# A two-layer encoder on one core: its scan in chunks of 64, with one matrix per unit made beforehand

## The chip, the cores and the metric

The kernel runs on one core of one Trainium2 chip. The metric is the device time of one execution in microseconds, median of the runs; beside it stands one profiled execution, whose trace is quoted here. The engines are PE (TensorE: matrix products into PSUM; PEld is its weight load), DVE (VectorE), ACT (ScalarE), POOL (GpSimd) and SP, which issues the DMAs.

## The reference

Input and output are 512 positions of 1024 features in float32. Layer 0 normalises, projects to seven groups of features, mixes them by a short convolution and by a 128x128 matrix over positions per group, gates, and projects back. Layer 1 normalises, projects, and has two mixers: a recurrence (forward and backward, 16 heads of 64 features) and a Fourier transform with a linear map; both are gated and projected back, and a last normalisation ends it. The change touches the recurrence alone:

```python
def wkv7_step(state, inp):
    r, w, k, v, a, b = inp
    sa = jnp.einsum('...ij,...j->...i', state, a)
    state = (state * w[..., None, :] + sa[..., :, None] * b[..., None, :]
             + v[..., :, None] * k[..., None, :])
    y = jnp.einsum('...ij,...j->...i', state, r)
    return state, y
...
    init = jnp.zeros((2, bsz, C_HEADS, C_HEAD_DIM, C_HEAD_DIM), jnp.float32)
    xs = (to_scan(r), to_scan(decay), to_scan(k), to_scan(v), to_scan(-kk), to_scan(kk * a))
    _, y = lax.scan(wkv7_step, init, xs)
    y = jnp.moveaxis(y, 0, 2)
    y_sum = y[0] + jnp.flip(y[1], axis=1)
    out = layer_norm(y_sum, lnx_g.reshape(C_HEADS, C_HEAD_DIM),
                     lnx_b.reshape(C_HEADS, C_HEAD_DIM), GN_EPS)
```

## The kernel before, in words

**Order.** The code doesn't call the engines. Each part of the work is a generator (a strand) that yields instructions (`Op`) and the names of things that it waits for; `Plan.run` keeps a rough clock of each engine and always issues the instruction that could start first, of equals that of the strand with the lower rank. Each engine then runs its instructions in that order. The scan (`chain`) has rank 0 and is looked ahead into: `held` keeps engines free for it. The blocks of layer 1's input projection (`block`, 24 products of 512 columns for 128 features) are strands of rank 5, gated by the scan's progress so that they lie between its steps. All instructions are recorded at one line, L367 (L378 in the changed program), so the trace is read by tiles. Tiles come from rings (`get`, `free`): a strand waits until a place of its ring is free. The planner's `took` charges extra where float32 products give way to float32r ones.

**Dense products** are float32r, every operand split into a high and a low part, three products each (`mm3`): `pd_*`, `pe`, `po`. The products of the recurrence are float32, and the trace has two records for each.

**The recurrence** goes over head pairs j = 0 to 7: two heads on 64 partitions each. A unit is a head e of the pair and a direction d, so a pair has four units. The sequence is cut into chunks of C = 32 positions, 16 to a pair, 128 in all. What a pair needs is built while the pair before it is scanned:

- `prep`, `half` (L1014): decays E, and the operands `at`, `bk` (b and k beside each other, by chunk) and `ar` (a and r, one tile per unit and half of the sequence), the latter copied into place by ACT or DVE.
- `sc`: scores of b and k with a and r in a chunk (64x64 tiles, two of them in turn); `masked` (L1053) copies the part that is to be inverted into `M` and masks the rest into `ar`.
- `inverse` (L1127): DVE solves blocks of 16, one matrix to a lane, in 30 short multiplications and additions of `iA` and `iT`; PE joins two blocks to 32 (`iH`, `iTT`, 32x32 tiles).
- `turn` (L1193): PE transposes `bk` (`tb`), ACT copies it into `bs`. `fold` (L1219): the inverse times b (`fb`) and times scores (`fr`), copied back into `bs` and `ar`.

**The scan** (`chain`, L1262). X has, for each unit, 64 rows of state, 32 of corrections and 32 of values. One chunk is a round trip of two products and two DVE instructions:

```python
ops = [V.tensor_tensor(X, pa, ph[:, :, n:n + 1].to_broadcast([P, 4, 64]), ALU.mult)]
ops += [T.matmul(pb[self.uq(e, d), n % 2, :], ar[e][d][n // 8][:, n % 8, 0, :], X[:, 2 * e + d, :], start=True, stop=True) for e, d in ((0, 0), (0, 1), (1, 1), (1, 0))]
ops += [V.copy_predicated(X, self.umask, pb[:, n % 2:n % 2 + 1, :].to_broadcast([P, 4, 64]))]
```

after which `bs` times X (128x64 tiles) and the next values (`c_cen`, 64x32 tiles) go into `pab`, and `outs` multiplies X with `ar` into `py` (128x32 tiles). `outputs` (L1317) copies `py` out, transposes it (`pt`) and adds the directions. `post` normalises and gates.

**PSUM**: four buffers `d` for dense blocks, two `s` for the building, one `py`, one `pab`.

Of the kernel before, what the change touches and what calls it, by code (L numbers as in the profile page):

```python
# [24 lines left out]
C = 32  # L25
NCH = S // C

# rows of the parameter matrix: 128 features each
# [15 lines left out]
def lay_out(inputs):  # L44
    """The arrays of one launch: the inputs laid out in the order of their tiles, and constants of shapes."""
# [21 lines left out]
def tables():  # L67
    """Constants: they depend on shapes alone."""
# [5 lines left out]
    t["cen"] = np.tile(np.eye(64) - 1 / 64.0, (2, 1))  # L74
    r, q = p % 64 // C, p % C
    c = np.arange(C)
    lt, le = q[:, None] < c[None, :], q[:, None] <= c[None, :]
    masks = []
    for d in range(2):
        is_k = (r == 1 - d)[:, None]  # L80
        masks.append(np.concatenate([lt & is_k, le], 1))
    t["masks"] = np.concatenate(masks, 1)
    t["eye32"] = q[:, None] == c[None, :]
    t["halves"] = np.stack([p % 2 == 0, p % 2 == 1, q < 16], 1)
# [10 lines left out]
# tiles with parts that depend on nothing in each other: after how many elements the parts repeat, and their size  # L95
PARTS = {"x23": (2 * D, D), "h1_23": (2 * D, D), "bk": (P, 64), "sq": (2 * S, S), "E": (2 * NCH * (C + 1), NCH * (C + 1)), "vq": (2 * S, S),
         "xw": (2 * S, S), "bs": (2048, 512), "ar": (64, 32), "y": (S, 256)}


@functools.lru_cache(None)  # L100
def parts(at, dims, period, size):
    """The parts that an access touches."""
    found = {at}
    for step, n in dims:
        found = {(a + step * i) % period for a in found for i in range(n)}
    return sorted({a // size for a in found})


class Op:
    """An instruction that is not issued yet: its engine, its call, what it writes and reads, and about how long it takes."""  # L110

    def __init__(self, eng, name, call, a, kw):
# [6 lines left out]
        if eng == "PE":  # L119
            m, n = math.prod(aps[1].shape[1:]), math.prod(aps[2].shape[1:])  # L120
            k, self.round = aps[1].shape[0] / P, aps[1].dtype == F32R
            self.cols = n * k * m / P
            if name == "transpose":
                self.cols *= 2
                self.cost = 0.11
            elif self.round:
                self.cost = n / 2400
            else:
                self.cols *= 4
                self.cost = n / 600 if m == P else 2 * max(m, n) / 1200 if aps[0].start_partition() == 0 else m / 1200  # L130
# [5 lines left out]
        # of what touches a bank of PSUM, one engine waits for another  # L136
# [4 lines left out]
    def where(x):  # L141
        """What it depends on: a tile by quarters of the partitions; of some tiles, their two parts."""
# [3 lines left out]
        if name.startswith("pab"):  # L146
            name = "pa" if x.offset % 384 < 256 else "pb"
# [4 lines left out]
        kind = PARTS.get(re.match("h1_23|x23|[a-z]*", name, re.I)[0])  # L152
# [6 lines left out]
class Plan:  # L159
    """The order of the instructions of many strands, each in its own order: always the instruction that could  # L160
    start first by a rough clock of the engines, of equals the one whose strand matters most. Every engine
    then runs its instructions in this order."""

    TICK, WINDOW, BUSY, SOFT = 3.413, 3.2, 3050.0, 2600.0
    SAFE, URGE = {}, 0.3
# [4 lines left out]
    def __init__(self, tc, nc):  # L170
        self.tc = tc
        self.clock = dict.fromkeys(("PE", "ACT", "DVE", "Pool", "SP"), 0.0)
        self.clock.update(round=False, table=None)
        self.wrote, self.read, self.cols = {}, {}, {}
        self.strands, self.done, self.rings, self.recent = [], set(), {}, deque()
# [10 lines left out]
    def unit(*ops):  # L186
        """Instructions that stay together if they can."""
# [5 lines left out]
    def either(op, other, gain):  # L193
        """An instruction that another engine could do; it does if that ends sooner by more than gain."""
# [6 lines left out]
    def get(self, pool, shape, dt, tag, name, bufs):  # L201
# [196 lines left out]
class K:  # L398
# [665 lines left out]
    def sums(self, j):  # L1064
# [18 lines left out]
        if j > 2:  # L1083
            yield f"X{j - 3}_15"
# [565 lines left out]
```

## Time and profile before

| | |
|---|---|
| Runs, us | 1132.07 median of 3 (1130.79 to 1137.01) |
| Profiled execution, span, us | 1137.8 |
| PE / DVE / ACT / POOL busy | 97% / 62% / 49% / 19% |
| Layer 0 | 0 to 440 us |
| Ramp: layer 1 begins, the first pair is built | 440 to 537 us |
| Scan: 128 chunk steps | 537 to 1072 us |
| Tail: output projection | 1072 to 1138 us |

The span runs from the first to the last instruction of the profiled execution; it lies at the upper end of the runs, 0.5% over their median. Busy PE time includes the draining of products and whatever lies between one product's start and its own end, so PE can be busy and still not issue.

### The profile page before, as it was taken

The numbers are of one execution on the slowest core, as the hardware profiler recorded it, in microseconds if no ns is written. First come the engines' busy times: TensorE is split into PE (matmuls) and PEld (weight loads), VectorE is DVE, ScalarE is ACT, GpSimd is POOL, SyncE is SP. The second block draws the span as 40 slices with busy tenths as digits, with TensorE's granted clock in tenths as the row PEclk, the third lists the DMA queues.
The fourth block names the chain that finished last, engine by engine and source line by source line (L and its number), as shares of the span: only waits on it lengthen the run. The fifth ranks groups of instructions, "written<-read, shape, count | busy, mean of one in ns | idle before, by whom it ended". The sixth has DMA issues, their size and how long they took to land.

```text
span 1137.8 us, 29635 instructions
## 1 busy us (share of the span) xinstructions
PE 1100.6 (97%) x12984; PEld 831.9 (73%) x12984; DVE 707.8 (62%) x1325; ACT 558.7 (49%) x976; POOL 211.9 (19%) x225
## 2 busy tenths in 40 slices
PE   7999999999999999989999999999999999999997
PEld 6988888888888888666666666666656666676786
DVE  6374444434432358897678678788777787856543
ACT  6232222222221156977386485773935847445333
POOL 3021111011010014342113112223222231122100
PEclk9999999999999999999899999999989999999999
DMA  8222222222232332222001101101111111242142
GB/s 288 76 93 93 74 93 94 103 100 93 93 130 93 130 130 84 85 70 72 21 31 48 49 31 48 46 33 39 31 55 41 39 39 41 94 146 85 57 139 111
DMA packets 32610, 91.57 MB, mean 80 GB/s; under 512 B 4960, under 2 KB 7648, under 8 KB 32480
## 3 DMA queue, kind: packets, MB, share of 16 engines
q1 hardware_dynamic: 32480, 89.67, 22.7%
q8 instruction: 102, 1.67, 0.6%
q14 instruction: 28, 0.23, 0.1%
HBM read 81.73 MB, written 7.86 MB: 79 GB/s over the span
## 4 chain that ended last, share of the span: by engine, by line
PE 81%; DVE 8%; ACT 8%; issue 2%; POOL 1%; DMA 0%; SPq 0%; POOLq 0%; DVEq 0%
PE pab L367 9%; PE pe L367 7%; PE po L367 6%; PE pv L367 4%; PE pd_ub L367 4%; PE pd_zb L367 4%; PE pd_xa L367 4%; PE pd_ba L367 4%; PE pd_za L367 4%; PE pd_ca L367 4%; PE pd_k L367 3%; PE pd_zc L367 3%; PE py L367 3%; PE pd_r L367 3%; PE pd_v L367 3%; PE sc L367 2%
## 5 line engine op out<-in xcount | busy, mean ns | idle before, releaser
L367 DVE COPY_PREDICATED X<-umask,pab 128x256 f32<-128x256 uint8 x128 | 56.9, 445 | 53.9 <-PE pab L367 53.2
L367 DVE TENSOR_TENSOR X<-pab,ph 128x256 f32<-128x256 f32 x128 | 54.0, 422 | 44.2 <-PE pab L367 42.8
L367 PE MATMUL pe<-w_e,yh 128*128 128x512 f32 x256 | 81.3, 398 | 0.0
L367 PEld LDWEIGHTS pab<-X,bs 128*64 128x64 f32 x960 | 38.4, 139 | 39.2 <-issue 13.6
L367 PE MATMUL pab<-X,bs 128*64 128x64 f32 x960 | 55.2, 237 | 6.6 <-DVE X L367 6.6
L367 PEld LDWEIGHTS pe<-w_e,yh 128*128 128x128 f32 x256 | 48.0, 188 | 11.6
L367 PE MATMUL pd_zc<-hh,w_zc 128*128 128x512 f32 x128 | 54.3, 435 | 0.9 <-POOL w_zc L367 0.9
L367 PE MATMUL pd_k<-hh,w_k 128*128 128x512 f32 (+1 forms) x144 | 54.2, 409 | 0.0
L367 ACT COPY bs<-tb 64x256 f32<-64x256 f32 x122 | 44.8, 367 | 16.1 <-PE tb L367 14.5
L367 PE MATMUL pe<-w_e,yl 128*128 128x512 f32 x128 | 50.4, 393 | 0.0
L367 PE MATMUL py<-X,ar 128*32 128x64 f32 x1024 | 50.3, 227 | 0.0
L367 PE MATMUL pd_v<-hh,w_v 128*128 128x512 f32 x128 | 50.1, 423 | 0.0
L367 PE MATMUL pd_r<-hh,w_r 128*128 128x512 f32 x128 | 50.0, 425 | 0.0
L367 DVE TENSOR_TENSOR w_e<-wf_e,w_e 128x1024 fp32r<-128x1024 f32 (+1 forms) x18 | 19.0, 1076 | 48.1 <-ACT w_e L367 47.9
L367 DVE TENSOR_TENSOR ar<-sc,c_masks 64x512 f32<-64x512 f32 x64 | 43.9, 686 | 7.6 <-ACT M L367 6.3
L367 PE MATMUL pv<-w_pv,hh 128*128 128x256 f32 x256 | 47.6, 289 | 0.0
L367 PEld LDWEIGHTS pab<-X,ar 128*32 128x32 f32 x1024 | 20.4, 109 | 37.2 <-issue 12.8
L367 ACT CAST w_e<-wf_e 128x1024 fp32r<-128x1024 f32 (+1 forms) x19 | 16.9, 912 | 62.3 <-PE pe L367 54.4
L367 ACT COPY M<-sc 32x256 f32<-32x256 f32 x62 | 37.6, 607 | 16.9 <-PE sc L367 16.1
L367 PE MATMUL pab<-X,ar 128*32 128x64 f32 x1024 | 41.4, 234 | 4.4 <-DVE X L367 4.3
L367 PE MATMUL sc<-ar,bk 64*64 64x64 f32 x1024 | 44.6, 224 | 0.9 <-ACT bs L367 0.9
L367 PEld LDWEIGHTS sc<-ar,bk 64*64 64x64 f32 x1024 | 35.7, 134 | 10.1 <-issue 3.6
(337 smaller groups left out, 2963.3 us busy)
## 6 DMA issues: line engine op xcount, KB each, us to landing
wf_e<-in_w_eo SPq DMA_DIRECT2D x16, 512.0 KB, 3.2
wf_o<-in_w_oo SPq DMA_DIRECT2D x12, 512.0 KB, 4.2
wf_pv<-in_w_ev SPq DMA_DIRECT2D x8, 512.0 KB, 5.6
wf_ub<-in_w_e SPq DMA_DIRECT2D x8, 512.0 KB
wf_zb<-in_w_e SPq DMA_DIRECT2D x8, 512.0 KB, 3.3
wf_xa<-in_w_e SPq DMA_DIRECT2D x8, 512.0 KB
wf_ca<-in_w_e SPq DMA_DIRECT2D x8, 512.0 KB, 3.2
wf_za<-in_w_e SPq DMA_DIRECT2D x8, 512.0 KB
```

What stands on the lines that cost most here:

```text
L367: i = op.call(*op.a, **op.kw)
```

## The change

A chunk has C = 64 positions: eight to a pair, 64 in all. For each unit and chunk one 128x128 matrix is made beforehand (`gq`): its right half takes X to the next state, its left half takes X to the outputs. A step of the scan is one DVE multiplication, `G` times X and the next values into `pa`, and X times `G` into `py`, all on 128x64 tiles (`c_cen` is padded with zeros to 128 rows). The outputs come feature-major and summed over the directions in PSUM, so the transposition after the scan is gone. The copy of corrections (`COPY_PREDICATED`) is gone too.

The building changes: `scores` makes the matrix to invert (`sm`), then products of a with k and the state (`sa`) and of b with r and the state (`sz`), 128 columns wide; `inverse` goes one step further, joining two inverses of 32 to one of 64 (`iTB`, `iG`, `iTJ`); `fold` multiplies with the inverse (`sp`) and sums four terms into each G (`sg`). b, k and r stay in one tile `ops` with an identity behind them.

The planner now charges for a change of tile shape on PE and prefers to stay with the shape that it has. `SLACK`, in chunks, is 2 for 4. PSUM has three `d` and three `s` buffers; a pass that needs two `s` waits for both.

```diff
-C = 32
+C = 64
...
+            self.mode = tuple(next(x for x in (32, 64, P) if x >= y) for y in (aps[1].shape[0], P if name == "transpose" else m))
...
-            cost += 0.09 * (op.round and not clock["round"])
-            clock["round"] = op.round
-            if self.cols.get(int(t / self.TICK) - 1, 0.0) < 3060:
+            if op.mode != clock["mode"]:
+                cost += self.SWITCH
+            clock["mode"] = op.mode
+            if self.cols.get(int(t / self.TICK) - 1, 0.0) < self.COLD:
...
+        if op.eng == "PE" and op.mode != self.clock["mode"] and not s[3]:
+            at += self.STAY
...
-                lo = yield from self.get("ll", f"ll{j}_{d}")
+                lo = self.ll[d]
...
-                                         T.matmul(ps, lo[r], self.xw[d][r, i, :], start=False, stop=True))
+                                         T.matmul(ps, lo[:, i, :], self.xw[d][:, i, :], start=False, stop=True))
...
+    def scores(self, j):
+        T, V, g = self.T, self.V, self.g[j]
...
+        for m in range(8):
+            for b in range(2):
+                for e, d in self.units:
+                    x = at[d][self.cr(e), C * m:C * m + C].rearrange("p (h c) -> p h c", h=2)
+                    yield T.matmul(ps[e][self.quarter(d, b), m, :], self.chunk(j, d, e, 0, m)[:, 32 * b:32 * b + 32], x[:, ::-1, :] if b else x, start=True, stop=True)
+        for e in range(2):
+            yield self.copy(mt[:, 8 * e:8 * e + 8, :], ps[e])
...
+            for m in range(4):
+                for e, d in self.units:
+                    yield T.matmul(ps[d][self.half_(e), m, :], at[d][self.cr(e), C * (4 * h + m):C * (4 * h + m) + C], self.ahead(j, d, e, 1, 4 * h + m), start=True, stop=True)
+            for e in range(2):
+                yield V.tensor_tensor(am[:, e, :, 0:C], ps[e][:, :, 0:C], self.masks[:, None, 5 * C:6 * C].to_broadcast([P, 4, C]), ALU.mult)
+                yield self.copy(am[:, e, :, C:2 * C], ps[e][:, :, C:2 * C])
...
+                    yield T.matmul(ps[e][self.half_(d), m, :], self.chunk(j, d, e, 0, n), self.ahead(j, d, e, 2, 7 - n if d else n), start=True, stop=True)
...
+        for n in range(16):
+            for r in rows[1::2]:
+                yield T.matmul(pt[r, n, :], H[r, n, :], Dt[r, n, :], start=True, stop=True)
+        for q, r in enumerate(rows):
+            yield self.copy(Ti[r, :, q % 2 * 32:q % 2 * 32 + 32], ps[r])
...
+                yield T.matmul(ps[q, n, :], mt[r, n, 32:64], Ti[r, n, 0:32], start=True, stop=True)
...
+                yield T.matmul(ps[r, n, :], B[r, n, :], H[r, n, :], start=True, stop=True)
...
+                    yield T.matmul(ps[d][self.half_(e), m, :], Ti[self.half_(d), 8 * e + 4 * h + m, :], zz[self.half_(d), e, m, :], start=True, stop=True)
...
+                            same.append((ps[e][self.cr(e), u, :], self.ident[self.cr(e), self.cr(e)], x))
+                            same.append((ps[e][self.cr(e), u, :], am[self.half_(e), d, n % 4, C:C2], y))
+                            other.append((ps[e][self.sr(e), u, :], self.chunk(j, d, e, 1, n), x))
+                            other.append((ps[e][self.sr(e), u, :], am[self.half_(e), d, n % 4, 0:C], y))
+                for k in range(8):
+                    for q in ((0, 0), (1, 1), (0, 1), (1, 0)):
+                        out, l, x = todo[q][k]
+                        yield T.matmul(out, l, x, start=k == 0, stop=k == 7)
...
+                        yield V.tensor_tensor(G[:, e, u, 0:C], ps[e][:, u, 0:C], x, ALU.mult)
+                    yield self.copy(G[:, e, :, C:C2], ps[e][:, :, C:C2])
...
+                ops = [V.tensor_tensor(X, pa, ph[:, :, m:m + 1].to_broadcast([P, 4, 64]), ALU.mult)]
+                if m < NCH - 1:
+                    ops += [T.matmul(pa[self.cr(e), 2 * e + d, :], G[:, e, 2 * (m % 2) + d, C:2 * C], X[:, 2 * e + d, :], start=True, stop=True) for e, d in units]
+                    ops += value(m + 1)
+                for e, d in units:
+                    t = C * (NCH - 1 - m if d else m)
+                    ops.append(T.matmul(py[self.cr(e), t:t + C], X[:, 2 * e + d, :], G[:, e, 2 * (m % 2) + d, 0:C], start=m == 0 and d == 0, stop=m == NCH - 1 and d == 1))
...
-            dp, sp, yp, cp = (self.pool(ctx, name, n, PSUM) for name, n in (("dense", 4), ("short", 2), ("outs", 1), ("chain", 1)))
+            dp, sp, yp, cp = (self.pool(ctx, name, n, PSUM) for name, n in (("dense", 3), ("short", 3), ("outs", 1), ("chain", 1)))
```

The order on PE at a chunk step. In a row, the product's tile is left of the arrow, its inputs right of it, then the output's size (partitions x columns); x4 stands for four alike. Before, chunk 13 of the third pair (the second visit of that step; the first one, four products `pab<-X,ar`, stands six dense products ahead):

```order
L367 MATMUL pd_k_6855<-hh,w_k_6749 128x512
L367 MATMUL pab<-X_13_6886,bs_3280 64x64 x4
L367 MATMUL pab<-c_cen,vq_5412 32x64 x4
L367 MATMUL py_8_6779<-X_13_6886,ar_011_5406 32x64
L367 MATMUL py_8_6779<-X_13_6886,ar_111_5408 32x64
L367 MATMUL py_8_6779<-X_13_6886,ar_001_5405 32x64
L367 MATMUL py_8_6779<-X_13_6886,ar_101_5407 32x64
L367 MATMUL pd_k_6855<-hh,w_k_6748 128x512
```

Now, chunk 2 of the fourth pair, PE again:

```order
L378 MATMUL za_1_6721<-xw_3336,ll_105 128x512
L378 MATMUL pa<-X_2_6727,gq_01_6581 64x64 x4
L378 MATMUL pa<-c_cen,vq_5038 64x64 x4
L378 MATMUL py_6582<-gq_01_6581,X_2_6727 64x64 x4
L378 MATMUL sz_00_6713<-ops_3233 64x128
L378 MATMUL sz_00_6713<-ops_3241 64x128
L378 MATMUL sz_01_6714<-ops_3233 64x128
L378 MATMUL sz_01_6714<-ops_3241 64x128
```

The visit with X and `ar` is gone, the twelve products that are left have one tile shape, and what stands behind them are products of the next pair's building rather than dense ones.

The order on PE in the building of the second pair, before, where the joint `iTT` is made:

```order
L367 MATMUL pab<-X_5_4684,ar_100_3450 32x64
L367 MATMUL iTT_4788<-iHs_4681,iDt_4661 32x32 x26
L367 MATMUL pab<-X_5_4684,bs_3224 64x64 x4
L367 MATMUL pab<-c_cen,vq_3295 32x64 x4
L367 MATMUL iTT_4788<-iHs_4681,iDt_4661 32x32 x19
L367 MATMUL pd_r_4631<-hh,w_r_4369 128x512
L367 MATMUL pd_r_4631<-hl,w_r_4369 128x512
L367 MATMUL pd_r_4631<-hh,w_r_4370 128x512
```

Now, the second pair again (`dz` is the inverse, `iB` and `iG1s` are copies out of PSUM, `ss` the sums of squares of the pair after):

```order
L378 MATMUL iTT_5149<-iHs_4762,iDt_4746 32x32 x64
L378 MATMUL iTB_5150<-iDt_4746,iHs_4762 32x32 x32
L378 MATMUL iG_5260<-dz_3253,mt_4361 32x32 x32
L378 MATMUL iTJ_5301<-iG1s,iB_5257 32x32
L378 MATMUL ss_5306<-sq_5240,ones 32x256 x2
L378 MATMUL iTJ_5301<-iG1s,iB_5257 32x32 x31
L378 MATMUL ss_5306<-sq_5240,ones 32x256 x2
L378 MATMUL sp_00_5351<-zz_0_4672,dz_3253 64x128
```

A pass that was cut into pieces by scan steps and dense products now runs whole, and passes that read each other's results stand behind each other.

## Rows read from the trace of the kernel before

**Rows 1.** The page's engine shares: busy us (share of the span), instructions.

```profile
PE 1100.6 (97%) x12984; PEld 831.9 (73%) x12984; DVE 707.8 (62%) x1325; ACT 558.7 (49%) x976; POOL 211.9 (19%) x225
```

**Rows 2.** Engine time by stretch: us; busy and count per engine; clock, DMA, GB/s.

```profile
0.00:440.00 440.00, 430.84 (x2147) 363.56 (x2148) 199.79 (x265) 137.01 (x191) 56.42 (x61) 1.00 0.32 111
440.00:537.00 97.00, 91.59 (x1016) 66.36 (x1015) 82.91 (x149) 76.31 (x144) 30.22 (x34) 1.00 0.23 80
537.00:1072.00 535.00, 518.91 (x9567) 354.28 (x9567) 397.98 (x872) 318.12 (x600) 123.64 (x129) 0.98 0.15 51
```

**Rows 3.** Waits in 537 to 1072 us: who for whom, us in total, times, longest.

```profile
DVE X L367 <- PE pab L367: 96.0, 152, 2.4
...
PE pab L367 <- DVE X L367: 10.9, 13, 1.8
PE iTT L367 <- DVE iHs L367: 2.2, 2, 1.8
```

**Rows 4.** PE in order of time, 703 to 707 us: start, length, what, count.

```profile
703.01 0.40 PE L367 MATMUL pd_v<-hl,w_v 128*128 128x512 f32 x1
703.24 0.39 PE L367 MATMUL pd_v<-hh,w_v 128*128 128x512 f32 x1
703.57 0.32 PE L367 MATMUL pab<-X,ar 128*32 128x64 f32 x8
703.81 0.50 PE L367 MATMUL pd_k<-hh,w_k 128*128 128x512 f32 x1
704.16 0.39 PE L367 MATMUL pd_k<-hl,w_k 128*128 128x512 f32 x1
...
705.07 0.40 PE L367 MATMUL pd_k<-hh,w_k 128*128 128x512 f32 x1
705.40 0.45 PE L367 MATMUL pab<-X,bs 128*64 128x64 f32 x8
705.78 0.32 PE L367 MATMUL pab<-c_cen,vq 64*32 64x64 f32 x8
706.03 0.42 PE L367 MATMUL py<-X,ar 128*32 128x64 f32 x8
706.38 0.51 PE L367 MATMUL pd_k<-hh,w_k 128*128 128x512 f32 x1
706.73 0.40 PE L367 MATMUL pd_k<-hl,w_k 128*128 128x512 f32 x1
```

**Rows 5.** PE in order of time: unbroken passes, each with the row behind it.

```profile
512.66 2.08 PE L367 MATMUL sc<-ar,bk 64*64 64x64 f32 x64 [0.86 <-ACT bs L367]
514.67 0.49 PE L367 MATMUL zw<-xw,lh 128*128 128x512 f32 x1
...
567.46 0.45 PE L367 MATMUL py<-X,ar 128*32 128x64 f32 x16
567.72 0.31 PE L367 MATMUL pab<-X,ar 128*32 128x64 f32 x8
569.72 0.66 PE L367 MATMUL tb<-c_ident,bk 128*128 128x128 f32 x4
...
723.35 1.10 PE L367 MATMUL fb<-bs,Ti 32*32 32x64 f32 x64 [0.92 <-ACT Ti L367]
724.37 0.50 PE L367 MATMUL pd_r<-hh,w_r 128*128 128x512 f32 x1
728.42 0.75 PE L367 MATMUL fr<-ar,Ti 32*32 32x32 f32 x64 [0.41 <-ACT bs L367]
729.10 0.51 PE L367 MATMUL pd_zc<-hh,w_zc 128*128 128x512 f32 x1
```

**Rows 6.** DVE groups: shapes, count, busy us, mean ns, idle before and releaser.

```profile
L367 DVE COPY_PREDICATED X<-umask,pab 128x256 f32<-128x256 uint8 x128 | 56.9, 445 | 53.9 <-PE pab L367 53.2
L367 DVE TENSOR_TENSOR X<-pab,ph 128x256 f32<-128x256 f32 x128 | 54.0, 422 | 44.2 <-PE pab L367 42.8
L367 DVE TENSOR_TENSOR ar<-sc,c_masks 64x512 f32<-64x512 f32 x64 | 43.9, 686 | 7.6 <-ACT M L367 6.3
```

More of the change, by code (lines that the diff above doesn't have):

```diff
@@ L220, in free, with both @@
         next(s for s in self.rings[tag] if s[0] is not None and s[0].tensor.name == t.tensor.name)[1] = True
+    def both(self, tag):
+        ring = self.rings.get(tag)
+        while ring and sum(s[1] for s in ring) < 2:
+            yield tag, "both", ring, 2
     def credit(self, tag, n):
@@ L298, in settle @@
                             break
-                    elif not (w in self.done if isinstance(w, str) else any(x[1] for x in w[2])):
+                    elif not (w in self.done if isinstance(w, str) else sum(x[1] for x in w[2]) >= w[3]):
                         break
@@ L479, in splits @@
             if key.startswith("pv") and key.endswith("_0"):
[L480 to L481 removed]
+                at = []
+                for tag in ("G", "ops"):
+                    at.append((tag, (yield from self.get(tag, f"w{tag}_{key}", shape, F32R))))
+                tiles = [t for _, t in at]
             elif key in (f"o0_{OUTS[-1]}", f"o1_{OUTS[-2]}"):
@@ L996, in build @@
             yield f"prep{j}_0"
-            g["bk"] = yield from self.get("bk", f"bk{j}")
+            g["ops"], g["at"], g["G"] = [], [None, None], []
+            for d in range(2):
+                g["ops"].append((yield from self.get("ops", f"ops{j}_{d}")))
             g["sq"] = yield from self.get("sq", f"sq{j}", [P, 2, S])
@@ L1182, in inverse @@
-        Ti = g["T"] = yield from self.get("Ti", f"Ti{j}")
-        for n in range(NCH):
-            for q in range(4):
-                r = slice(32 * q, 32 * q + 32)
-                yield T.matmul(ps[r, n, :], Dt[r, n, :], H[r, n, :], start=True, stop=True)
+        yield from self.plan.both("s")
+        ps = yield from self.get("s", f"iTT{j}", [P, 16, 32])
+        pt = yield from self.get("s", f"iTB{j}", [P, 16, 32])
+        for n in range(16):
+            for r in rows:
+                yield T.matmul(ps[r, n, :], Dt[r, n, :], H[r, n, :], start=True, stop=True)
@@ new lines, in inverse @@
+        B = yield from self.get("Dn", f"iB{j}", [P, 16, 32])
+        for r in rows[1::2]:
+            yield self.copy(B[r], pt[r])
+        self.free("s", pt)
+        ps = yield from self.get("s", f"iG{j}", [P, 16, 32])
+        for n in range(16):
+            for d in range(2):
+                r, q = rows[2 * d], rows[2 * d + 1]
+                yield T.matmul(ps[q, n, :], mt[r, n, 32:64], Ti[r, n, 0:32], start=True, stop=True)
+        self.free("q", mt)
+        H = yield from self.get("F", f"iG{j}s", [P, 16, 32])
@@ new lines, in inverse @@
+        for r in rows[1::2]:
+            yield self.copy(H[r], ps[r])
+        self.free("s", ps)
+        ps = yield from self.get("s", f"iTJ{j}", [P, 16, 32])
+        for n in range(16):
+            for r in rows[1::2]:
+                yield T.matmul(ps[r, n, :], B[r, n, :], H[r, n, :], start=True, stop=True)
+        for r in rows[1::2]:
+            yield self.copy(Ti[r, :, 0:32], ps[r])
+        self.free("s", ps)
+        self.free("Dn", B)
+        self.free("F", H)
+        self.plan.done.add(f"tt{j}")
@@ L1259, in unit_states @@
-        self.plan.done.add("bs")
+        for tag, n in (("ops", 4), ("dz", 2)):
+            got = []
+            for i in range(n):
+                t = yield from self.get(tag, f"{tag}{i}")
+                got.append(t)
+                if tag == "dz":
+                    yield self.G.memset(t, 0.0)
+                else:
+                    for e in range(2):
+                        yield self.G.tensor_copy(t[self.cr(e), 3 * S:], self.ident[self.cr(e), self.cr(e)])
+            self.plan.keep.add(tag)
+            self.free(tag, *got)
```

556 lines of the change are left out of this document (255 added, 301 removed).

## The prediction

> **What bounds the kernel now.** I read the page's line of engine shares first: PE (TensorE) is busy 97% of the 1137.8 us span, DVE 62%, ACT 49% [rows 1]. An average hides stages, so next the table of engine time by stretch [rows 2]. Layer 0 (0 to 440 us) is dense 512-column products; the ramp (440 to 537) makes the first head pair ready; the scan (537 to 1072) is 128 chunk steps with layer 1's projections and the building of the next head pair between them; the tail is dense again. PE is busy 518.9 of 535 us in the scan, DVE 398.0. Third, the waits [rows 3]. DVE waits 96.0 us for PE's `pab`, PE only 10.9 us for DVE's X: the recurrence looks serial, but the engine that ends its wait is nearly always PE, and PE is working through its queue. So the scan's time is a sum of PE time, and halving the number of steps by itself buys nothing. What counts is the PE time that is removed and added.
>
> Fourth, how this PE time is spent, in the order of time [rows 4]. Dense products follow each other every 0.23 us (703.01 to 703.24). At 703.57 a visit of four scan products (128x32 tiles) comes between two dense blocks: from the last dense start, 703.24, to the second dense start after it, 704.16, are 0.92 us. Two dense products are 0.46 of it and the four scan products 0.13 (below); 0.33 go to two changes of tile shape. The second visit of that step, at 705.40, has three shapes: from 705.07 to 706.73 are 1.66 us, less 0.46, less 0.55 for its twelve products, which leaves 0.65 for four changes, 0.16 each. The stretch from 705.78 to 706.03, 0.25 us for four products and one change, gives 0.12. I take **0.15 us a change**, with 0.12 and 0.165 as ends. This is what a row doesn't name: the engine counts as busy there.
>
> **What one small product costs.** From unbroken passes, start to next start, less one change of 0.15 where one stands [rows 5] (two records are one float32 product). Scores `sc`, 64 columns on two tiles: (2.01 - 0.15) / 32 = 0.058 us. `fb`, 64 columns on four tiles: (1.02 - 0.15) / 32 = 0.027. `fr`, 32 columns on four tiles: (0.68 - 0.15) / 32 = 0.017. `py` with eight products in a row on four column tiles: 0.26 / 8 = 0.0325. One tile thus takes about 0.117 us for 64 columns and 0.066 for 32, whatever else runs, and the price is that over the number of different tiles in turn. 128 columns don't occur on small tiles; from 32 to 64 columns 0.05 comes on top, so 0.21 at the least by that slope, 0.234 by doubling; I take 0.22, or 0.055 on four tiles and 0.11 on two. A transposition: four in 0.66, the last end trailing by 0.17 as the dense rows' do, so 0.12.
>
> **The change part by part.** Counts are instructions of the two programs.
>
> *Removed products*: `sc` 512 x 0.058 = 29.7; `fb` 512 x 0.027 = 13.8; `fr` 512 x 0.017 = 8.7; 128 `tb` and 64 `pt` transpositions x 0.12 = 23.0; the scan's `pab<-X,ar` 512 x 0.0325 = 16.6, `pab<-c_cen` 512 x 0.03 = 15.4, `pab<-X,bs` 480 x 0.058 = 27.8, `py` 512 x 0.05 = 25.6 (mostly on two tiles). Sum 161 us.
>
> *Added products*: `sg` 1024 on four tiles x 0.055 = 56.3; `sz` and `sp` 512 x 0.055 = 28.2; `sa` 256 on two tiles x 0.11 = 28.2; `sm` 512 x 0.022 = 11.3 (0.017 to 0.029, four tiles or more); the joints `iTB`, `iG`, `iTJ` 768 on two tiles x 0.033 = 25.3 (0.017 to 0.066, four tiles or one); `pa` 480 and `py` 256 x 0.058 = 42.7. Sum 192 us. So the arithmetic costs **+31 us**: folding more beforehand is more work, not less.
>
> *Changes of tile shape*: 979 in the program before, 309 after. A chunk step had up to six of them, at 128 steps; now its twelve products have one shape (128x64), at 64 steps, and the planner keeps equal shapes together; the 64-row LoRA products are padded to 128 and change nothing any more. 670 x 0.15 = **-100 us** (-80 to -111).
>
> *Waits.* Before, all idle PE time of the scan is 535 - 518.9 = 16 us. After, a head pair is built in 15 passes (`sm`, two `sa`, two `sz`, `iH`, `iTT` with `iTB`, `iG`, `iTJ`, two `sp`, four `sg`), and most read what DVE or ACT takes out of PSUM after the pass before. The price of such a hop with nothing under it is that of `iTT` waiting for `iHs`: 2.2 us in two waits, 1.1 each [rows 3]. In the new order dense blocks cover most; bare are some six in the first pair, where the dense blocks have run out, and one or two in each other pair (the `iG`, `iTJ`, `sp` rows of the change's section). 18 x 1.1 = **+20 us**; the ends are 0 (as tight as now) and +70.
>
> *Beside the path.* DVE loses COPY_PREDICATED 56.9, half of the X multiplications 27.0 and the `ar` masks 43.9 [rows 6], and gets 64 masks of 256 columns at the X row's 0.42 = 27 and 128 of 128 columns, which lie under that price, at most 54: it falls, and stays under PE, which covers it at some 74% as now. ACT loses its copies into `bs`, `ar` and `M`. Eight small loads a pair for `nss` instead of two stand in SP's queue ahead of weights; what waits for them is the inverse of a pair, with the dense blocks of the ramp and a whole pair's period over it, and the weights are three slabs ahead: nothing, while those covers last; if the first inverse started 2 or 3 us later, the ramp would pay that once. Three dense PSUM buffers for four: a block lasts 24 x 0.23 = 5.5 us, so each buffer has two blocks' time to be emptied; nothing. The transform's last two groups now wait for the last chunk; the output projection's other blocks lie over that.
>
> **Sum.** 1137.8 + 31 - 100 + 20 = 1089 us for a profiled execution. The median of the runs before is 1132.07, 0.995 of the profiled span, so 1089 x 0.995 = **1083 us**.
>
> **The rivals.**
>
> *Tiles that share rows work one after the other* (slower). `sg`, `sz` and `sp` count on four 64x64 tiles at once, two on the same 64 rows. If those two took turns, 1536 products would cost 0.11 and not 0.055: +84, so 1173 x 0.995 = 1167 us. For it: no 64x64 pass of the trace has more than two tiles, on different rows. Against it: `pab<-c_cen` has two 64x32 tiles on each half of the rows, and its four products take 0.25 with their change [rows 4], a quarter of one tile's time each. It decides from 0.10 us per product on, where it eats the gain. The Trainium skill ("TensorE: Matmul & The Clock Gate", section on packing small matmuls) says that a weight load overlaps running matmuls only where the row group differs. By that rule this rival would be the forecast and `c_cen` could not be at a quarter; the trace disagrees with it there, which is why its chance is small: 0.07.
>
> *The hops come bare* (no change, or slower). PSUM's three small buffers are taken two at a time, and each must be emptied by DVE and ACT before the pass after next. If ten of a pair's 15 hops were bare, 8 x 10 x 1.1 = 88 instead of 20: 1157, or 1151 us. It decides from some eight bare hops a pair (69 us). For it: the passes are longer and the dense blocks between them come in runs of 24 rather than of 3, so that cover lies in fewer places. Against it: the same planner leaves PE 16 idle us in the scan now, with 14 such passes a pair. The skill ("TensorEngine Tiling", PSUM Bottleneck) warns of this: tiling speeds up the products, not the emptying, which may become the bound. Here DVE and ACT get less to empty, so by the rows it is latency alone that could cost. Chance 0.10, of which 0.04 within half a per cent.
>
> *The scan's latency was the bound after all* (much faster). Then 64 steps of one hop in place of 128 of two would give hundreds of us. PE's 10.9 us of waiting for X speak against it; the most that could be had of all PE waits in the scan is 16 us. With no bare hop at all: 1069, or 1064 us. That is inside my range; below it I leave 0.05, for better-packed `sa` and joints.
>
> *The change doesn't do what it says*: if the order had as many shape changes as before. The counted order excludes it; that a change costs 0.12 rather than 0.15 is in the range.
>
> **How the numbers follow.** Forecast with its bounds 0.78; below 1045 us 0.05; bare hops 0.10; tiles in turn 0.07. Bounds around 1083: changes +20/-11, columns and joints +30/-20, waits +50/-20; they don't fall together, so 1045 to 1130 us holds about 8 in 10, leaving the upper end of the hops and the tile rival out. Half a per cent of 1132 is about what a measurement of this kernel can tell from no change: faster 0.83, same 0.04, slower 0.13.
>
> **What would show it.** Right: `sg` in runs of 32 products at 1.8 us; chunk visits of twelve products at 0.7 us plus two changes; PE's idle time in the scan at 20 to 40 us; DVE under 80% there; the scan some 50 us shorter while layer 0 and the tail keep their length. Wrong: `sg` runs at 3.5 us (tiles in turn); `iTJ`, `sp` or `sg` high in PE's list of waits with ACT or DVE behind them (bare hops); a ramp much longer than 97 us; or a granted clock at its lower level (1.2 GHz) for long in the stretches without dense blocks.

## The result and the profile after

The changed kernel takes 1176.47 us (median of 4, 1171.82 to 1177.8) against 1131.43 us: **1.0355 times as long**, 95% interval 1.0306 to 1.0405. (The kernel before has one run more here than in the table ahead.) Forecast were 1083 us and a range of 1045 to 1130. The profiled execution spans 1176.0 us.

The page of the kernel after, engine shares (as [rows 1]) and the granted clock in 40 slices, and below it the clock of the kernel before in its own 40 slices:

```profile
PE 1084.0 (92%) x13304; PEld 881.3 (75%) x13304; DVE 657.1 (56%) x1246; ACT 469.7 (40%) x759; POOL 170.2 (14%) x212
...
PEclk9999999999999999989989999889899998978999
```

```profile
PEclk9999999999999999999899999999989999999999
```

PE is less busy in a longer span (1084 of 1176 us, 1100.6 of 1137.8 before), and its clock, nearly whole before, has dips from about 500 us on. Engine time by stretch, which answers to [rows 2]: layer 0, ramp, scan (the first X at 539, the last at 1123.5), tail; columns: window, us, busy (and count) of PE, PEld, DVE, ACT, POOL, clock, DMA share, GB/s:

```profile
0.00:440.00 440.00, 427.58 (x2122) 359.60 (x2123) 195.59 (x255) 134.77 (x189) 58.19 (x63) 1.00 0.33 110
440.00:539.00 99.00, 91.23 (x1132) 71.48 (x1132) 69.53 (x120) 55.25 (x88) 19.71 (x31) 0.95 0.26 81
539.00:1124.00 585.00, 519.66 (x9856) 413.68 (x9854) 369.13 (x836) 257.62 (x444) 91.02 (x118) 0.93 0.16 51
1124.00:1176.00 52.00, 45.50 (x202) 36.55 (x202) 22.81 (x37) 22.09 (x38) 1.28 (x1) 0.98 0.31 107
```

Layer 0 is as before; the ramp has 99 us instead of 97, at a clock of 0.95 instead of 1.00. The scan has 585 us instead of 535; PE is busy as long in it (519.7 and 518.9), idle 65 us instead of 16, and the clock there is 0.93, not 0.98. The tail has 52 us instead of 66: of the output projection's 288 products, 192 stand behind the last X instead of 256, so some 14.7 us of dense work (64 x 0.2295) that lay in the tail now lie in the scan. The waits of PE in the scan (as [rows 3]: who for whom, us in total, times, longest):

```profile
PE sa L378 <- ACT gq L378: 8.1, 7, 2.5
PE sg L378 <- issue: 6.8, 6, 1.7
PE iTB L378 <- issue: 6.8, 4, 2.5
PE pa L378 <- DVE X L378: 6.6, 9, 1.9
PE sz L378 <- ACT gq L378: 6.3, 7, 1.0
PE sg L378 <- ACT gq L378: 4.3, 5, 2.7
PE iTJ L378 <- issue: 3.2, 2, 1.7
```

The recurrence (`pa` for X) is not the reason: 6.6 us, less than the 10.9 before. New are waits within the building (of 64.5 us, 20.6 stand under "issue", where the profile names no releaser). `sa` and `sz` don't read `gq` at all: what they wait for is that ACT has copied `gq` out of the PSUM buffer that they are to write. One such place, PE in order of time:

```profile
686.79 0.37 PE L378 MATMUL sg<-pt,am 64*64 64x128 f32 x4
686.90 0.27 PE L378 MATMUL sa<-ops,at 64*64 64x128 f32 x1
686.99 0.28 PE L378 MATMUL sg<-pt,am 64*64 64x128 f32 x3
687.01 0.27 PE L378 MATMUL sa<-ops,at 64*64 64x128 f32 x1
689.78 2.82 PE L378 MATMUL sa<-ops,at 64*64 64x128 f32 x22 [2.51 <-ACT gq L378]
692.54 0.64 PE L378 MATMUL pa<-c_cen,vq 128*64 128x64 f32 x8
```

DVE and ACT at the same time:

```profile
686.90 1.97 DVE L378 TENSOR_TENSOR iA<-iL,nr 128x256 f32<-128x256 f32 x2
688.80 0.47 DVE L378 TENSOR_TENSOR gq<-sg,c_masks 128x128 f32<-128x128 f32 x2
...
689.36 0.37 ACT L378 COPY gq<-sg 128x256 f32<-128x256 f32 x1 [2.10 <-DVE gq L378]
```

And the stretches before and behind it (us, PE busy, clock, DMA share, GB/s):

```profile
686.20:689.60 3.40, 1.08 (x40) 0.99 0.03 7
689.60:693.00 3.40, 3.21 (x30) 0.50 0.27 88
```

`sa` follows `sg` at once. Its first product has the third `s` buffer; the second needs one that `sg` has just filled. DVE is in the long multiplications of the next inverse (`iA`) until 688.80, ACT copies after DVE, and PE stands for 2.5 us. Then the granted clock is 0.50, its lower level (1.2 GHz), for 3.4 us, and the next 11 products of `sa` (22 records) take some 0.24 us each instead of 0.109: half speed. The profile after has 13 such stretches ahead of its last 2 us, 89 us together; the one before has three, 24 us.

**An account.** Three words first. A *pass* is the run of small products that one step of the building puts into its PSUM buffers; a *hop* is the way of its result from PE to DVE or ACT and back; a wait of PE is *bare* where no other product is there to be done under it. To compare kernels I gave each product from 440 us on its price in unbroken passes (dense 0.2295 us, `sg` 0.055, `sa` 0.109, `pa` 0.0585 and so on), once more where the clock was at its lower level ("lower clock"); what is left between two starts goes to a change of tile shape where there is one, and is a wait above 0.25 us (above 0.45 at a change, 0.15 of it staying with the change). The account divides all of the time, so its terms add up by construction; how much falls to each depends on the prices. "Close" counts, in the order of the program, building passes with fewer than four dense products since the pass before.

| us from 440 us on | products | changes of shape (count) and rest | waits | lower clock | sum | close |
|---|---|---|---|---|---|---|
| before | 497.0 | 160.5 (979) | 23.9 | 9.4 | 690.7 | 57 of 112 |
| after | 536.5 | 60.6 (309) | 95.8 | 36.2 | 729.0 | 101 of 128 |
| difference | +39.5 | -99.9 | +71.9 | +26.8 | +38.3 | |
| forecast | +31 | -100 | +20 | none | -49 | |

So the changes came out as forecast and the arithmetic 8.5 us above it; the waits and the clock ate the gain. (The sums differ by 38.3 us, the medians by 45.0: the profiled execution of the kernel before lies at the upper end of its runs.)

### The profile page after: what moved, and what is told of

Read it like the earlier page. It is cut to its first block, busy times and chain, and to the rows that moved or that the text cites. A ratio compares the mean times of both kernels' runs of the same rounds, so it can differ in the third digit from the quotient of the medians.

```text
span 1176.0 us, 29938 instructions
## 1 busy us (share of the span) xinstructions
PE 1084.0 (92%) x13304; PEld 881.3 (75%) x13304; DVE 657.1 (56%) x1246; ACT 469.7 (40%) x759; POOL 170.2 (14%) x212
## 4 chain that ended last, share of the span: by engine, by line
PE 75%; DVE 14%; ACT 5%; issue 4%; DMA 1%; POOL 1%; SPq 0%; DVEq 0%; ACTq 0%; POOLq 0%
PE pe L378 7%; PE po L378 6%; PE pd_zb L378 4%; PE pd_ub L378 4%; PE pd_xa L378 4%; PE pd_ba L378 4%; PE pd_za L378 4%; PE pd_ca L378 4%; PE pd_v L378 3%; PE pd_zc L378 3%; PE pd_r L378 3%; PE pd_k L378 3%; PE pv L378 3%; PE sg L378 3%; PE sa L378 3%
## 5 line engine op out<-in xcount | busy, mean ns | idle before, releaser
L378 PE MATMUL sg<-ops,c_ident 64*64 64x128 f32 x512 | 65.1, 277 | 9.0 <-ACT gq L378 4.3
L378 PE MATMUL sg<-pt,am 64*64 64x128 f32 x1024 | 63.7, 271 | 2.3 <-issue 2.3
L378 PEld LDWEIGHTS sg<-ops,c_ident 64*64 64x64 f32 x512 | 46.2, 132 | 19.0 <-issue 8.6
L378 PE MATMUL sa<-ops,at 64*64 64x128 f32 x512 | 48.6, 313 | 10.1 <-ACT gq L378 8.1
L378 PE MATMUL sg<-ops 64*64 64x128 f32 x512 | 52.4, 276 | 2.4 <-issue 2.4
L378 PEld LDWEIGHTS sg<-pt,am 64*64 64x64 f32 x1024 | 50.7, 133 | 3.3 <-issue 2.8
L378 PEld LDWEIGHTS sa<-ops,at 64*64 64x64 f32 x512 | 38.3, 154 | 15.2 <-ACT gq L378 9.9
L378 PE MATMUL pd_zb<-hh,w_zb 128*128 128x512 f32 x128 | 40.4, 392 | 0.0
L378 PE MATMUL pd_ub<-hh,w_ub 128*128 128x512 f32 x128 | 40.4, 392 | 0.0
L378 PE MATMUL pd_xa<-hh,w_xa 128*128 128x512 f32 x128 | 40.4, 392 | 0.0
L378 PE MATMUL pd_ba<-hh,w_ba 128*128 128x512 f32 x128 | 40.4, 392 | 0.0
```

What stands on the lines that cost most here:

```text
L378: i = op.call(*op.a, **op.kw)
```

## The experiments

The charges for a change of tile shape stand in one line of the planner: SWITCH makes its clock count a change, STAY puts a product of another shape off by 0.15 us in its choice. All kernels but e7 and e8 are the changed kernel with the edit shown. An edit to the planner or its buffers moves the order of the whole program; the number of changes and "close" say how far. Their accounts ("close" was counted for some):

| run | us | ratio to before (95%) | changes | waits | lower clock | close |
|---|---|---|---|---|---|---|
| after | 1176.5 | 1.0355 (1.031 to 1.041) | 309 | 95.8 | 36.2 | 101 |
| e1: 2 `d`, 4 `s` | 1134.1 | 0.998 (0.996 to 1.001) | 269 | 68.0 | 29.3 | 98 |
| e2: 4 `d`, 2 `s` | 1272.6 | 1.122 (1.116 to 1.128) | 280 | 158.7 | 71.5 | |
| e3: no charges | 1123.9 | 0.991 (0.988 to 0.995) | 456 | 36.7 | 15.2 | 48 |
| e4: URGE turned round | 1154.7 | 1.018 (1.013 to 1.023) | 280 | 82.2 | 34.4 | |
| e5: e3 with 2 `d`, 4 `s` | 1160.0 | 1.021 (1.019 to 1.024) | 406 | 62.7 | 33.7 | |
| e6: e3 with 4 `d`, 2 `s` | 1199.1 | 1.055 (1.052 to 1.057) | 465 | 73.4 | 49.7 | |
| e9: SWITCH alone | 1121.9 | 0.988 (0.985 to 0.992) | 426 | 34.2 | 14.4 | |
| e10: STAY alone | 1175.5 | 1.035 (1.029 to 1.042) | 288 | 96.7 | 31.5 | 96 |
| e11: e3, true costs | 1120.4 | 0.986 (0.981 to 0.990) | 453 | 35.5 | 14.5 | |
| e12: e3, longer hops | 1120.2 | 0.987 (0.983 to 0.991) | 499 | 27.4 | 15.2 | |
| e13: STAY, small products | 1210.6 | 1.066 (1.064 to 1.068) | 299 | 124.1 | 46.2 | 108 |
| e14: STAY, dense products | 1130.6 | 0.995 (0.993 to 0.997) | 399 | 47.5 | 20.4 | 46 |
| e15: SWITCH, costs, hops | 1115.4 | 0.981 (0.978 to 0.985) | 450 | 32.7 | 13.6 | 48 |
| e16: e13, costs, hops | 1192.1 | 1.048 (1.045 to 1.051) | 339 | 105.1 | 36.0 | |

### Buffers: e1, e2

```diff
+    def lend(self, a, b):
+        yield "n1_3"
+        t = yield from self.get(a, "lent")
...
+        self.plan.strand(1, self.lend("d", "s"))
```

From layer 1 on one `d` buffer becomes an `s` buffer (e2: `lend("s", "d")`). The first half of the last output projection takes its four buffers to match: two `d` and two `s` in e1, four `d` in e2, three `d` and one `s` in the changed kernel.

> The changed kernel, but from layer 1 on one PSUM buffer goes from the dense blocks to the building: two `d` and four `s` instead of three and three. Theory A (in the changed kernel PE waits 96 us from 440 us on, start to start, against 24 before, since a building pass that needs two of three `s` buffers waits until DVE and ACT have emptied the pass before; after such a wait the granted clock falls to 1.2 GHz): with four buffers a pass can start while the one before it is emptied; PE's waits fall by 25 to 45 us, the time at the lower clock (92 us) with them, and the kernel takes 1110 to 1150 us. Theory B (the waits are those of results, not of buffers: a pass reads what DVE or ACT make of the pass before): waits stay within 10 us, 1165 to 1180 us. Theory C (the dense blocks are the scarce ones): two `d` buffers make blocks wait, 1180 us or more.

> The changed kernel with PSUM split as in the kernel before: from layer 1 on four `d` and two `s` buffers. Theory A (the building waits for its PSUM buffers): every pass of two buffers waits until both are emptied, about 1 us at 12 passes of each of 8 pairs; waits grow by 30 to 80 us, 1200 to 1260 us. Theory B (results, not buffers): within 10 us of 1176. Theory C (dense blocks scarce): faster than 1170.

1134.1 and 1272.6 us: with the charges on, a buffer more saves 42 us, a buffer less costs 96. Theory A held on both sides (e2 beyond its 1260); B and C fall. In the account e1's 42 us are 28 of waits, 7 of lower clock and some 6 of its 40 fewer changes; of the 72 us of added waits 44 remain, so buffers are a part of them. PE's waits in e2 name the buffers:

```profile
PE sz L381 <- ACT am L381: 16.2, 20, 2.5
PE sg L381 <- ACT gq L381: 14.9, 16, 1.4
PE sa L381 <- ACT zz L381: 12.0, 12, 2.9
```

None of the three reads what it waits for: each is the copy that empties a buffer. The Trainium skill ("TensorEngine Tiling (Array Packing)", section PSUM Bottleneck) says that after products are packed the copying out of PSUM may become the bound. These rows agree, but ACT is busy only 37% of e2's span, so it is the latency of the copies that counts here and not their load.

### Order: e3, e4

```diff
-    SAFE, URGE, SWITCH, STAY, COLD = {}, 0.3, 0.2, 0.15, 1800.0
+    SAFE, URGE, SWITCH, STAY, COLD = {}, 0.3, 0.0, 0.0, 1800.0
```

(e4 has URGE -0.3 and the charges as they were.)

> The changed kernel with the planner's two charges for a change of tile shape set to 0 (as in the kernel before): PE changes its tile shape 451 times instead of 307. Theory A (buffers): the 144 changes cost 144 x 0.15 = 22 us; PE's waits fall a little as dense products are mixed in, by 10 to 30 us: 1165 to 1190 us. Theory D (the planner's wish to stay with one shape puts passes behind each other and leaves their hops bare): waits and lower clock fall by more than the changes cost, 1110 to 1150 us.

> The changed kernel with the planner's preference for dense products turned round (URGE -0.3 instead of 0.3): dense products come when nothing else can start, instead of ahead of everything whenever PE has done few columns lately. Theory E (dense blocks are spent in unbroken runs of 24 to 47 products, and are not there when a pass waits): waits fall by 20 to 50 us, 1120 to 1155 us. Theories A and B: the dense work of a pair is the same, waits within 15 us, 1160 to 1190 us.

e3 takes 1123.9 us, 52.6 less than the changed kernel, though it has 147 changes of shape more: those cost 30 us in the account (91.1 against 60.6), and waits and clock give back 59 + 21. That was theory D. The number of changes sets a limit to what the charges are worth: without them the changed kernel still has 523 changes fewer than the kernel before (456 for 979). In e3 dense products lie between the joints, PE in order of time:

```profile
641.96 1.20 PE L378 MATMUL iG<-dz,mt 32*32 32x32 f32 x64
643.09 0.50 PE L378 MATMUL pd_k<-hh,w_k 128*128 128x512 f32 x1
...
645.03 0.40 PE L378 MATMUL pd_k<-hh,w_k 128*128 128x512 f32 x1
645.36 0.24 PE L378 MATMUL iTJ<-iG2s,iB 32*32 32x32 f32 x2
645.53 0.50 PE L378 MATMUL pd_k<-hh,w_k 128*128 128x512 f32 x1
```

Between `iG` and `iTJ`, which needs its copy, PE works 2.3 us on a block. e4 saves 22 us with 13.6 us fewer waits: its time (1154.7) lies at the end of theory E's range, its waits within that of A and B, so that dense products are preferred is at most a lesser part.

### Both at once: e5, e6

> Both edits that helped alone: the two charges for a change of tile shape at 0 and two `d`, four `s` buffers from layer 1 on (404 changes of tile shape). If scarce buffers and stacked passes are two causes that add up: waits fall from 37 us (without the charges) to 15 to 25, changes cost 52 x 0.15 = 8 us less than there, 1095 to 1112 us. If they are one cause (stacked passes are what makes the buffers scarce), the second edit brings only its fewer changes: 1112 to 1125 us.

> The charges at 0 with four `d` and two `s` buffers, the split of the kernel before (460 changes of tile shape). With the charges this split cost 96 us. If the buffers are scarce in themselves (a pass of the changed kernel fills two of them whatever stands between the passes): 1180 to 1230 us. If they are scarce only because the passes are stacked: 1120 to 1150 us.

Both expectations of e5 were wrong: 1160 us, slower than either edit alone. Its waits:

```profile
PE iTB L381 <- issue: 9.5, 5, 2.4
PE zw L381 <- DVE rq L381: 4.3, 1, 4.3
PE pd_zd L381 <- DVE zg L381: 4.2, 1, 4.2
PE po L381 <- DVE fd L381: 3.7, 1, 3.7
```

The first row names no releaser, as in the changed kernel. The others are new: dense products that wait, up to 4.3 us at once, until DVE has emptied a buffer. So where dense products lie between the passes, two `d` are too few. With two `s` (e6) the time is 1199, between its two expectations and 75 us above e3, but its largest row is of another kind, since `ss` reads the `sq` that it waits for:

```profile
PE ss L381 <- ACT sq L381: 10.3, 4, 4.7
```

Of the three splits, three and three is the fastest in the mixed order, and two `d` and four `s` in the stacked one (e1). That dense blocks need fewer buffers there, as they run whole, is my reading; no run shows it by itself. What a buffer is worth hangs on the order.

### The price of a bare wait: e7, e8

```diff
         ps = yield from self.get("d", f"pd_{kind}{q}")
...
+        a, b = self.pz
+        B = self.T.matmul(ps[:, 0:8], self.ident, a, start=True, stop=True)
+        B.keys = [], []
+        yield self.plan.unit(*(x for _ in range(4) for x in (self.V.tensor_copy(b, a), self.A.copy(a, b))), B)
```

This is the kernel before, with a product ahead of each block that waits for a chain of copies; in e8 the product reads `self.ident[:, 0:8]` instead of `a`.

> The kernel before with bare waits added: ahead of each of 39 dense blocks of layer 1 stands a small product (128x8, into the block's own PSUM buffer, which the block then starts anew) that waits for a chain of eight copies of 8 columns between DVE and ACT. Measured against the next kernel, in which the same product and the same copies are there but the product doesn't read them. Each wait should last 1 to 2.5 us, 40 to 100 us in all. If a wait costs its own length only: the difference is the sum of the waits that the trace shows. If the granted clock falls after it (Theory A): about 0.3 to 0.5 of that on top, and time at the lower clock grows from 27 us to 60 to 130 us.

> The control of the run before: the kernel before with the 39 small products and the chains of copies, the product reading a constant instead. Expected 1135 to 1150 us (39 products of about 0.1 us, and 312 copies on DVE and ACT beside PE's work), the clock as in the kernel before.

1291.5 and 1235.1 us. From 440 us on, e7 and then e8 (us, busy and count per engine, clock, DMA share, GB/s):

```profile
440.00:1288.60 848.60, 734.80 (x10918) 516.09 (x10918) 548.09 (x1220) 443.78 (x930) 170.92 (x170) 0.89 0.15 50
```

```profile
440.00:1233.70 793.70, 714.86 (x10916) 503.26 (x10915) 549.48 (x1223) 444.57 (x931) 171.80 (x170) 0.93 0.16 54
```

PE is idle 113.8 us in e7 and 78.8 in e8, and the clock is 0.89 and 0.93. The waits meant are there, 27 of them with 57.9 us, one as long as 7.9 us where 2.5 was expected at most; the largest row of them:

```profile
PE pd_r L367 <- ACT pz L367: 19.0, 7, 6.7
```

Others shrink under them, so in the account waits grow by 37.9 us (82.3 to 120.2). Lower clock grows by 19.9 (41.7 to 61.6). Together that is 57.8, where the profiled spans are 54.9 apart and the medians 56.5: **in this pair a microsecond of bare wait costs a half on top.** Over the other runs, each against the kernel before, lower clock grows by 0.30 (e10) to 0.49 (e9) for each microsecond of waits; only e5, e6 and e12, the last with just 3.5 us more waits, have more. The Trainium skill ("TensorE: Matmul & The Clock Gate", section on psum-queue depth-cycling) describes such a thing: short idle spells between groups of products, from cycling through PSUM, make the clock go to and fro. These runs agree: the granted clock of e7 falls to 0.5 in 24 separate stretches, 183.5 us together, and that of e8 in 18, 114.4 us (the last us of the program included, as in the expectation's 27 us before).

The control missed its expectation by 85 us, in its clock too, and that tells something of the kernel before:

```profile
PE pab L367 <- DVE X L367: 34.9, 38, 3.1
```

312 copies of 8 columns stand in DVE's and ACT's queues, X comes later, and PE's wait for X rises from 10.9 us [rows 3] to 34.9. That is 24 of the 58 us of added waits; the recurrence was not the bound of the kernel before, but this suggests little slack there.

### Which charge: e9, e10

> One of the two charges alone: SWITCH 0.2 (the planner's clock counts a change of tile shape), STAY 0 (it doesn't put a change off): 421 changes. If the putting off is what stacks the passes, this is as the run without both (1124 us) less 30 changes at 0.15: 1110 to 1130 us. If the charge in the clock does it: 1155 to 1180.

> The other charge alone: SWITCH 0, STAY 0.15: 286 changes of tile shape, as few as with both. If the putting off stacks the passes: waits of 80 to 110 us, 1155 to 1185 us. If it is the charge in the clock: 1100 to 1130.

1121.9 and 1175.5 us: STAY alone brings the whole difference between e3 and the changed kernel, SWITCH changes nothing that the intervals can tell from e3.

### By which way: e13, e14

```diff
-        if op.eng == "PE" and op.mode != self.clock["mode"] and not s[3]:
+        if op.eng == "PE" and op.mode != self.clock["mode"] and not s[3] and not s[4]:
             at += self.STAY
...
-                at = t - self.URGE + (self.STAY if op.mode != self.clock["mode"] else 0.0)
+                at = t - self.URGE
```

(`s[3]` marks the strand of the scan, `s[4]` those of dense products. e14 has `and s[4]` instead of `and not s[3]` in the first line and keeps the second.)

> The changed kernel, with STAY for small products alone: a dense product may break in at no charge. 296 changes of tile shape. If passes are bare because dense products are kept from coming between them: waits fall to 30 to 50 us, 1110 to 1135 us. If they are bare because small passes queue up on each other whatever dense products may do: 1155 to 1180 us.

> The counterpart: STAY for dense products alone, small passes change shapes at no charge. 394 changes. If dense products kept off are the cause: as the changed kernel, 1155 to 1180 us (394 - 307 changes cost 13 of it). If small passes queued on each other are: 1105 to 1130 us.

1210.6 us (e13, above both of its expectations) and 1130.6 (e14, at the upper end of its second). My first idea, that dense products are kept out, falls: freed alone they don't help. With STAY on the small products the loss is there, without it nearly all of it is gone. STAY makes small products follow each other: `sa`, `sz`, `sp` and `sg` have one shape, 64x64, and two buffers each, and 108 of 128 passes come close behind another (46 in e14). PE's largest wait in e13 is again for the emptying of `sg`:

```profile
PE sa L378 <- ACT gq L378: 11.8, 7, 3.3
```

Why e13 is 34 us worse than the changed kernel, with a like order of passes, is not settled.

### Versions: e11, e12, e15, e16

```diff
-                self.cost = n / 600 if m == P else 2 * max(m, n) / 1200 / {(P, 64): 2, (P, 32): 4, (64, 64): 4, (64, 32): 6}.get(self.mode, 4)
+                tiles = 2 if re.match("sa|iTB|iG|iTJ", aps[0].tensor.name) else {(P, 64): 2, (64, 32): 6}.get(self.mode, 4)
+                self.cost = n / 600 if m == P else 2 * max(m, n) / 1200 / tiles
...
-    LATE = {"": 0.2, "PE": 0.25, "ACT": 0.2, "DVE": 0.3, "Pool": 0.3, "SP": 2.5}
+    LATE = {"": 0.2, "PE": 0.5, "ACT": 0.4, "DVE": 0.5, "Pool": 0.5, "SP": 2.5}
```

e11 has the first edit on e3, e12 the second; e15 has both with SWITCH 0.15 and STAY 0, e16 both on e13.

> No charges, and the planner's cost of `sa` and of the joints `iTB`, `iG`, `iTJ` doubled, as the trace has them (two tiles at once, not four: `sa` 0.109 us a product where the planner had 0.053). A version meant to beat both kernels: its clock is late by some 29 us less. If the remaining waits (37 us) come of a wrong clock, they fall by 10 to 20: 1100 to 1118 us. If not: 1118 to 1130.

> No charges, and the planner's delay between two engines raised from 0.2-0.3 to 0.4-0.5 us, so that it puts other work under a hop for longer; 495 changes of tile shape instead of 451. If the remaining waits are hops that the planner takes for shorter than they are: waits fall from 37 to 15-25 us, the clock's share with them, less 44 x 0.145 = 6 us for the changes: 1105 to 1120 us. If not: 1125 to 1140.

> A version meant to beat both: SWITCH 0.15, STAY 0, the costs of `sa` and the joints as the trace has them, the delay between engines 0.4 to 0.5 us. 446 changes. If the three help by different ways they add up: e9, e11 and e12 are 2, 3.5 and 4 us under the run without charges, so 1108 to 1118 us; if they are within what two orders differ by chance: 1115 to 1130.

> As e13, with the costs and delays of e15: 336 changes of tile shape. If few changes and few waits can be had together: 100 changes fewer than e15 are 15 us, 1095 to 1110 us. If the waits come back as changes are saved: 1125 to 1160 us.

1120.4, 1120.2, 1115.4 and 1192.1 us. All three without STAY lie below the kernel before. e11's waits are those of e3 (35.5), so the few microseconds between them may be chance; e12's fall to 27.4, though not to the 15 to 25 expected, and its 43 changes more eat most of that. e15 beats both kernels, 1.9% under the one before (1.55 to 2.16%); its 1115.4 lies in both of its expected ranges, so whether its parts add up can't be told. e16 gives the answer that the forecast needed, and misses both of its ranges (1192.1 us): with STAY on small products, 111 changes fewer than in e15 come with 72 us more waits.

## Why the prediction was wrong

**Right.** The prices. A pass of 32 `sg` products takes 1.76 us (543.39 to 545.30 less a change of 0.15; 1.8 was forecast), a chunk visit 0.70 (548.74 to 549.59 less 0.15; 0.7 was forecast), each of 16 `sa` products 0.112 ((1.94 - 0.15) / 16; 0.11 was forecast). PE in order of time, two records to a product:

```profile
511.95 2.02 PE L378 MATMUL sa<-ops,at 64*64 64x128 f32 x32
513.89 1.29 PE L378 MATMUL iH<-iD,off 32*32 32x32 f32 x128
...
543.39 0.33 PE L378 MATMUL sg<-ops,c_ident 64*64 64x128 f32 x2
...
544.97 0.40 PE L378 MATMUL sg<-pt,am 64*64 64x128 f32 x8
545.30 0.73 PE L378 MATMUL bo<-hi,ones 128*128 128x512 f32 x2
...
548.74 0.45 PE L378 MATMUL pa<-X,gq 128*64 128x64 f32 x8
549.02 0.40 PE L378 MATMUL pa<-c_cen,vq 128*64 128x64 f32 x8
549.26 0.40 PE L378 MATMUL py<-gq,X 128*64 128x64 f32 x8
549.59 1.52 PE L378 MATMUL sa<-ops,at 64*64 64x128 f32 x22
```

That settles the rival of tiles that take turns: four 64x64 tiles, two on the same rows, run at 0.055 us a product (`sg`), half of the 0.11 of two tiles on different rows (`sa`). The rule of the Trainium skill ("TensorE: Matmul & The Clock Gate", section on packing small matmuls) that a weight load overlaps products only on other rows would give twice that; the trace disagrees. Products came to +39.5 us for +31, changes of shape to -99.9 for -100. DVE fell (369 us of the scan, 63%), the ramp is 99 us, layer 0 is as long; the scan's latency is no bound. Of the signs of being right, three failed: PE's idle time in the scan is 65 us and not 20 to 40, the scan is 50 us longer and not shorter, and the tail did not keep its length (52 us for 66).

**Wrong: the step on waits.** "18 x 1.1 = **+20 us**" had the right price and the wrong number. Waits grew from 32 (23.9 us) to 102 (95.8 us), 0.94 us each in the mean: 70 more, not 18. The forecast counted the bare hops in a few places of the order and took the rest for covered ("dense blocks cover most"); against the rival of bare hops it held that "the same planner leaves PE 16 idle us in the scan now". It was not the same planner: it now puts changes of shape off, and that stacks the passes. The forecast took its saving on changes and its small waits for independent, and they were not. Of the 670 changes saved, 523 (69 us in the account) come without any charge, as e3 shows; the charges save the other 147 (30 us) and cost 59 us of waits and 21 us of lower clock. So no run has both of the forecast's terms: e3 and e9 have 36.7 and 34.2 us of waits, under the forecast's 44, but 456 and 426 changes; the changed kernel has 309 changes and 95.8 us. Without the stacking the time comes to 1124 us (e3), at the upper end of the forecast's range. The order could have told of the stacking beforehand: 101 of 128 passes come close behind another, 57 of 112 before, 48 of 128 in e3.

**Wrong: no term for the clock.** Behind some of the bare waits the products run at 1.2 GHz, and what that costs grew from 9.4 to 36.2 us: +26.8. The prediction named a lower clock as a sign, but neither its sum nor its rival on bare hops had a price for it. The trace before has three stretches at the lower level (at 542.6, 829.3 and 942.0, behind waits of 1.5 to 1.8 us), which would have given one. That rival (72 us in the account, 88 in the text) was the right one; with the clock its 1151 us become 1178. That this is so near to the measured 1176 is in part luck: its waits were 16 us too high, the products 8.5 too low. It got a chance of 0.10.

With the terms as measured, 1137.8 + 39.5 - 99.9 + 71.9 + 26.8 = 1176.1 us; the profile has 1176.0.

**Open.** What `iTB` waits for: 6.8 us in the changed kernel and 8.4 in e15 stand under "issue", with no releaser. The further loss of e13. And what the other edits to the planner are worth that came with the change (`SLACK`, `COLD`, the costs of some products): no run varies the first two.

## What to carry to other kernels

Fewer changes of tile shape are worth their price (0.15 us each here) only if the order that saves them leaves independent work between a pass and the next one that needs its buffer or its result: count the passes with nothing in between before crediting the saving. Price a bare wait of PE at its length and, in kernels like these, a third to a half as much again for the clock. And what a PSUM buffer is worth depends on the order: moving one from the dense blocks to the small passes gave 42 us in one order and cost 36 in another.

## What the hardware showed that was not expected

In the changed kernel the granted clock fell after waits of 0.8 to 2.5 us between passes that kept PE busy otherwise, and stayed at its lower level (1.2 GHz) for 3.4 to 17 us. It did not fall after every such wait: one of 2.7 us, at 858.6, had no fall behind it, and there are 13 stretches for 102 waits. Nor is it the order alone that decides. The 34 executions of the kernel before that were timed beside the experiments have one and the same order, and their mean clock goes from 0.999 (spans of 1128.7 to 1129.3 us) to 0.987 (1139.2 us); a term for the clock of some 10 us can come and go between two executions of one program.

Tiles of 64x64 on the same rows work at the same time: 0.055 us a product on four tiles, 0.11 on two. And 312 copies of 8 columns, with 39 small products, made the kernel before 8.6% slower (e8). DVE and ACT are busy 41 and 23 us longer for them, and PE's waits grow by 58 us (24 of them for X) and its lower clock by 32; which of the copies delays what is not shown beyond X.
